# Quadrant swap of a matrix by HBM-to-HBM copies: a short first DMA and a small-packet last DMA on each queue

## Chip, cores, metric

One core of a Trainium2 chip. Times are device microseconds of that core. The runs of one job share a chip. The kernel before took 811.68 us in the median of the first three runs (811.56 to 812.05).

## The reference

```python
def setup_inputs():
    return {"x": np.random.randn(8192, 8192).astype(np.float32)}

def reference(x):
    return np.fft.ifftshift(x)
```

With even sizes this swaps the four quadrants: the upper left one with the lower right one, the upper right one with the lower left one. No arithmetic is done: 268.44 MB are read from HBM and 268.44 MB written.

## The kernel before

```python
STEP = 8
hr, hc = R // 2, C // 2
dims = [[STEP * C, hr // STEP], [1, hc]]        # 512 half rows of 16 KB, every eighth row
for c in range(STEP):
    for col in (0, hc):
        for eng, r0, h in ((nc.sync, 0, col), (nc.scalar, hr, hc - col)):
            eng.dma_start(
                out=bass.AP(out.tensor, out.offset + (r0 + c) * C + h, dims),
                in_=bass.AP(x.tensor, x.offset + (hr - r0 + c) * C + hc - h, dims),
            )
```

SP's queue (q1 in the profile) writes the upper half of the output, ACT's queue (q10) the lower half, 16 DMAs of 8 MB each. No data passes through SBUF. A few words that come again: an issue is the instruction with which SP or ACT hands a DMA to its queue; a packet is what one of the 16 DMA engines moves at a time, here one half row of 16 KB; a completion count is the 4-byte packet with which an engine reports that its share of a DMA is done; landing is when all 16 have; the plateau is the steady rate in the middle of the run.

## Time and profile before

| of the first trace of the kernel before | |
|---|---|
| time, median of 3 unprofiled runs | 811.68 us |
| the profiled execution itself | 823.08 us, span 821.3 us |
| DMA engines' busy share | over 0.9 in 39 of 40 slices |
| 16 KB packet, mean (packet records) | 801 ns, never under 608 |
| first packet / last packet's end | 2.10 / 820.11 us |

The lines themselves stand in the prediction. Read them in three steps: which of the 16 DMA engines' time is empty (the DMA row), how much of the span lies before the first and after the last packet (the stretches), and whether a wait for an earlier DMA keeps an engine from its next packet (the packet records: each packet starts about 4 ns before the one ahead of it ends, so none does).

### The profile page before, as it was taken

Reading aid. Unit: us, or ns where it says so; the run is one execution under the profiler, and the core shown is the slowest. Engines: PE = TensorE matmul, PEld = TensorE weight load, DVE = VectorE, ACT = ScalarE, POOL = GpSimd, SP = SyncE. Lnnn points to the kernel's source line nnn. Section 1 sums busy time; section 2 is a strip of 40 time slices with the busy share of each in tenths; the row PEclk is TensorE's granted clock in tenths of the full one; section 3 lists DMA queues with packets and bytes.
Section 4 is the critical chain, followed back from the end, with each engine's and each line's share of the span. In section 5 each row is a group of like instructions: output and inputs, shape, how many; then the busy total and the mean of one; then the engine's idle time right before and its main releaser. Section 6 shows DMA issues by size and latency. Waiting matters only on the chain. (4 is left out here: it accounts for less than half of the span.)

```text
span 821.3 us, 77 instructions
## 1 busy us (share of the span) xinstructions
POOL 0.2 (0%) x4
## 2 busy tenths in 40 slices
POOL 0000000000000000000000000000000000000000
DMA  9999999999999999999999999999999999999998
GB/s 304 325 328 333 326 325 330 321 329 330 325 330 330 327 328 333 329 330 330 328 328 327 334 325 330 326 326 328 331 329 330 326 332 326 328 324 333 326 328 298
DMA packets 16896, 268.44 MB, mean 327 GB/s; under 512 B 512, under 2 KB 512, under 8 KB 512
## 3 DMA queue, kind: packets, MB, share of 16 engines
q1 hardware_dynamic: 8448, 134.22, 50.2%
q10 hardware_dynamic: 8448, 134.22, 49.7%
HBM read 268.44 MB, written 268.44 MB: 654 GB/s over the span
## 5 line engine op out<-in xcount | busy, mean ns | idle before, releaser
L51 POOL MEMSET const-bfloat16-1.0<- 128x1 bf16 x1 | 0.1, 103 | 0.0
L51 POOL MEMSET const-uint8-127<- 128x1 uint8 x1 | 0.1, 102 | 0.0
L51 POOL MEMSET const-float32-0.0<- 128x1 f32 x1 | 0.1, 99 | 0.2 <-issue 0.2
L51 POOL MEMSET const-float32-1.0<- 128x1 f32 x1 | 0.1, 99 | 0.0
## 6 DMA issues: line engine op xcount, KB each, us to landing
out_dram<-in_x_dram ACTq DMA_DIRECT2D x16, 8192.0 KB, 204.3
out_dram<-in_x_dram SPq DMA_DIRECT2D x16, 8192.0 KB, 204.1
```

Of the source, the lines that this page charges most:

```text
L51: nc = _bacc.Bacc("TRN2", target_bir_lowering=False, num_devices=1)
```

## The change

The intent is to start data moving sooner with a DMA of one row per DMA engine, and to end more evenly with finer packets. Everything between stays.

```diff
-    dims = [[STEP * C, hr // STEP], [1, hc]]
+    def copy(eng, r0, row, n, h, limit=None):
+        dims = [[STEP * C, n], [1, hc]]
+        kw = {"max_dma_last_dim": limit} if limit else {}
+        eng.dma_start(out=..., in_=..., **kw)       # addresses as before, cut here
+
+    full = hr // STEP
     for c in range(STEP):
         for col in (0, hc):
             for eng, r0, h in ((nc.sync, 0, col), (nc.scalar, hr, hc - col)):
-                eng.dma_start(...)
+                if (c, col) == (0, 0):
+                    copy(eng, r0, c, 16, h)
+                    copy(eng, r0, c + 16 * STEP, full - 16, h)
+                elif (c, col) == (STEP - 1, hc):
+                    copy(eng, r0, c, full - 32, h)
+                    copy(eng, r0, c + (full - 32) * STEP, 32, h, 2048)
+                else:
+                    copy(eng, r0, c, full, h)
```

More of the change, by code (lines that the diff above doesn't have):

```diff
@@ L10 @@
 STEP = 8
+PARTS = 16
 @with_exitstack
@@ L27 @@
     hc = C // 2
-    dims = [[STEP * C, hr // STEP], [1, hc]]
+    def copy(eng, r0, row, n, h, limit=None):
+        dims = [[STEP * C, n], [1, hc]]
+        kw = {"max_dma_last_dim": limit} if limit else {}
+        eng.dma_start(
+            out=bass.AP(out.tensor, out.offset + (r0 + row) * C + h, dims),
+            in_=bass.AP(x.tensor, x.offset + (hr - r0 + row) * C + hc - h, dims),
+            **kw,
+        )
+    full = hr // STEP
     for c in range(STEP):
@@ L32 @@
             for eng, r0, h in ((nc.sync, 0, col), (nc.scalar, hr, hc - col)):
-                eng.dma_start(
-                    out=bass.AP(out.tensor, out.offset + (r0 + c) * C + h, dims),
-                    in_=bass.AP(x.tensor, x.offset + (hr - r0 + c) * C + hc - h, dims),
-                )
+                if (c, col) == (0, 0):
[6 more added lines that the diff above has]
+                    copy(eng, r0, c, full, h)
 _INS = ['x']
```

## The prediction

> **What bounds the kernel now.** I read the page first, for which engine is busy, then the stretches at the two ends, then the waits of the queue that closes the program, then the issue times. No compute engine does anything here: the program is 32 copies from HBM to HBM, 16 on each of two queues, so the rows of the DMA engines are the profile.
>
> Of the page of the kernel before (one digit and one GB/s figure for each fortieth of the span, some 20.5 us each):
>
> ```profile
> span 821.3 us, 77 instructions
> DMA  9999999999999999999999999999999999999998
> GB/s 304 325 328 333 326 325 330 321 329 330 325 330 330 327 328 333 329 330 330 328 328 327 334 325 330 326 326 328 331 329 330 326 332 326 328 324 333 326 328 298
> DMA packets 16896, 268.44 MB, mean 327 GB/s; under 512 B 512, under 2 KB 512, under 8 KB 512
> q1 hardware_dynamic: 8448, 134.22, 50.2%
> q10 hardware_dynamic: 8448, 134.22, 49.7%
> HBM read 268.44 MB, written 268.44 MB: 654 GB/s over the span
> ...
> out_dram<-in_x_dram ACTq DMA_DIRECT2D x16, 8192.0 KB, 204.3
> out_dram<-in_x_dram SPq DMA_DIRECT2D x16, 8192.0 KB, 204.1
> ```
>
> The 16 DMA engines are at nine tenths or more in every slice but the last, and the two queues' packet time adds up to 50.2 + 49.7 = 99.9% of 16 engines. 16896 packets are 16384 of 16 KB (one half row each) and 512 of 4 bytes (32 DMAs by 16 engines, the completion counts). Only the first slice (304) and the last (298) are below the plateau of about 328; each loses roughly (328 - 304) / 328 x 20.5 = 1.5 us and (328 - 298) / 328 x 20.5 = 1.9 us. So an edit to the first and last DMA alone has about 3.4 us of profiled time to play for, and part of that is start and finish of the program itself.
>
> The stretches at both ends (length, POOL's busy time, clock, mean busy share of the DMA engines, GB/s; a packet is booked whole to the stretch in which it starts, so a share can exceed 1):
>
> ```profile
> 0.00:2.10 2.10, 0.20 (x4) 1.00 0.00 0
> 2.10:3.50 1.40, 0.00 (x0) 1.00 1.11 269
> 3.50:5.30 1.80, 0.00 (x0) 1.00 0.90 373
> 5.30:8.00 2.70, 0.00 (x0) 1.00 1.08 388
> 8.00:14.00 6.00, 0.00 (x0) 1.00 1.02 347
> ...
> 816.70:818.00 1.30, 0.00 (x0) 1.00 0.97 328
> 818.00:819.00 1.00, 0.00 (x0) 1.00 0.98 328
> 819.00:819.80 0.80, 0.00 (x0) 1.00 0.31 123
> 819.80:820.20 0.40, 0.00 (x0) 1.00 0.00 0
> ```
>
> Nothing moves before 2.10 us; from then on the engines are full until about 819. The packet records say it more finely: all 16 engines take a first packet between 2.10 and 2.70 us, and each starts its next packet about 4 ns before the one before has ended, with no hole in between. A 16 KB packet takes 801 ns in the mean and never under 608; 25% take exactly 611. After the last data packets the 16 engines end between 819.56 and 820.11, in the mean 819.76: the slowest is only 0.36 us behind the mean.
>
> The waits of the queue that closes the program, and the first issues:
>
> ```profile
> SPq L62 <- DMA out_dram<-in_x_dram: 167.2, 2, 118.8
> SPq L33 <- DMA out_dram<-in_x_dram: 133.8, 12, 50.6
> ```
> ```profile
> 0.73 50.48 ACTq L33 DMA_DIRECT2D out_dram<-in_x_dram  x4
> 0.73 45.43 SPq L33 DMA_DIRECT2D out_dram<-in_x_dram  x4
> ```
>
> Each queue issues four DMAs at once (the fourth blocks for 43 to 48 us, so the queue is full), and then waits for the one four back before each of the next 12. With some 200 us from issue to landing, against 51 us of work in one DMA, those waits are far ahead of the data. They cost nothing.
>
> **What the Trainium skill says.** The page "HBM Reference", Specifications, gives about 716 GB/s for an HBM domain. The profile has 654, read and write together: 91% of it, if both tensors lie in one domain, which no view shows. I take it as sign that the plateau is memory's, which the change does not touch. "DMA: Bandwidth & Descriptors", in the section on why a DMA increments its semaphore by 16, says that a hardware-queue DMA uses the largest number of engines up to 16 that divides its slowest dimension. The trace agrees: 512 completion packets for 32 DMAs. New outer sizes are 16, 496 = 16 x 31, 480 = 16 x 30 and 32, so all 16 engines stay in use with equal shares. The same page, "Why small descriptors are slow (HBM only)", gives about 3 cycles of overhead per packet. In the trace a 4-byte completion packet takes 9 ns, about 6 after the overlap: I use 6 ns. "Perfetto Trace Analysis", DMA Instruction, HWDGE, says that the profiled duration of an issue is descriptor generation, not movement. The trace agrees: the first SP issue lasts 0.58 us and its 8 MB land 51 us later.
>
> **The change, part by part.** The bytes, the queues and the order of rows stay. Each queue goes from 16 to 18 DMAs.
>
> 1. First DMA of one row per engine. Before, the first issue runs from 0.73 to 1.31 us (512 rows) and the first packet starts 0.79 later, at 2.10. If generation is proportional to rows, 16 rows take 0.58 x 16 / 512 = 0.02 us and the start is up to 0.56 us earlier. If it is a fixed cost, it is 0. The unblocked 512-row issues last 0.51 to 0.62 us (only DMAs of 512 rows exist, so the split can't be read). I take a bit over half: -0.30 us. This lies straight on the path, since all engines then run full to the end. The second DMA's descriptors come about 0.6 us after the first's; a first packet takes 1.2 to 1.5 us, so no hole opens.
>
> 2. Two more DMAs per queue: 2 x 2 more completion packets per engine, 4 x 6 ns = +0.02 us. Data packets just after a completion packet take 783 ns in the mean, the others 801, so there is no hidden stall. The two more issues run beside full engines: 0.
>
> 3. Last 32 rows of each queue in 2 KB packets. Per engine: 2 rows x 2 queues = 4 packets of 16 KB become 32 of 2 KB, 28 more by 6 ns = +0.17 us. They may also flow less well than 16 KB ones: these 64 rows are 1.05 MB, 3.2 us at 328 GB/s; I allow a further 5%, +0.16.
>
> 4. The end. A finer last packet can shorten the end by what the slowest engine lags, 0.36 us, at most, as rows stay bound to engines; and the drain after the last byte (last completion packet 820.11, its count seen at 820.44) stays. I take -0.15.
>
> Sum: -0.30 + 0.02 + 0.17 + 0.16 - 0.15 = -0.10 us. As the author of such an edit aims at the first and last slice, and as I cannot see the generator's split, I lean a little further to the good side: 811.68 - 0.10 - 0.3 = 811.3 us.
>
> **The rivals.**
> - *Small packets starve the tail.* If an engine can only keep a few packets in flight, 2 KB ones no longer cover the latency (a first packet takes about 0.7 us longer than the 611 floor). For: nothing in this kernel is below 16 KB but the counts. Against: counts flow through in 9 ns without a hole behind them. If the tail ran at half rate, +3.2 us: about 815.
> - *The start or the end is worth all it can be.* -0.56 at the start and -0.36 at the end, small packets free: about 810.8. For: the first slice's 304.
> - *The rows' phase changes the plateau.* With 16 rows split off, the engines' places in the second DMA (496 rows) and in the 480-row one may stand in another relation to each other, which memory may like more or less. These are about 6% of the bytes; a rate 5% up or down on them is 0.06 x 0.05 x 812 = 2.4 us either way, 809 to 814. For: packets of 611 ns beside ones of 925 (75th percentile) show contention, and at the start, with q1 alone (3.4 to 5.3 us), packets take 628 ns in the mean. Against: the plateau moves only between 321 and 334 whatever the drift.
> - *The queues' lead.* q1 is 4 packets per engine ahead at first, and q10 alone ends the run. With short first DMAs they may interleave sooner and end together. q10 alone still moves 328 GB/s, so no gain follows.
>
> **Range and chances.** The three runs spread over 0.5 us. Edges add from -0.9 to about +1 us, the phase up to 2 either way with small weight, a starved tail +3 with about one chance in ten. Predicted 811.3 us, 80% range 809.3 to 813.0. 2% is 16.2 us, five times all that both end slices lose: faster by over 2% has 1%, within 2% 98%, slower 1%.
>
> **What would show it.** First packets at 1.6 to 1.9 us instead of 2.10 would bear out step 1; at 2.1, a fixed issue cost. The packet counts should be 36 x 16 = 576 completion packets and 16384 - 64 + 512 = 16832 of data, 17408 in all, of which 1088 under 8 KB; other counts would mean that the DMAs are cut otherwise than I think. A last slice below 298 GB/s, or 2 KB packets well over 110 ns each, shows the starved tail; a plateau off 328 in slices 2 to 4 or in the last three shows the phase. I am wrong if the time leaves 809.3 to 813.0, above all if the middle of the run moves, where I say nothing changes.

## The result, and the profile after

The changed kernel took 811.86 us in the median of six runs (811.57 to 812.42), the kernel before 811.69 (811.40 to 812.15) in six runs. The ratio is 1.0002, with a 95% interval of 0.9989 to 1.0015: no difference. A ratio is the mean time of one kernel's fast runs over that of the other's fast runs of the same rounds, so it is not quite the ratio of the medians.

From the page of the changed kernel (span; GB/s in 40 slices; packets):

```profile
span 809.9 us, 81 instructions
...
GB/s 298 333 328 334 330 335 333 331 336 330 333 333 333 333 335 333 337 334 329 336 333 335 333 335 333 332 333 333 337 331 335 333 334 330 334 335 329 335 336 299
DMA packets 17408, 268.44 MB, mean 331 GB/s; under 512 B 576, under 2 KB 576, under 8 KB 1088
```

The packet counts are those that the prediction worked out. The two slices that the change aims at have not moved: 298 and 299 against 304 and 298. What differs is what the change does not touch: the slices between are at about 333 instead of 328, and the span is 11 us shorter, while the unprofiled times agree within 0.2 us. So this pair of traces must not be compared for its middle.

The first issues of the changed kernel (start, length of the chain of four issues, both in us), and the waits of SP's queue (total us, times, longest us):

```profile
0.73 2.60 SPq L32 DMA_DIRECT2D out_dram<-in_x_dram  x4
0.73 2.96 ACTq L32 DMA_DIRECT2D out_dram<-in_x_dram  x4
```
```profile
SPq L32 <- DMA out_dram<-in_x_dram: 187.7, 14, 50.1
SPq L75 <- DMA out_dram<-in_x_dram: 116.8, 2, 98.5
```

Four issues now fit into 2.60 us, because the fourth no longer finds the queue full: the four together hold 16 + 496 + 512 + 512 rows where they held 2048. The fifth blocks in its place, for 41.6 us. The first issue by itself, of 16 rows, lasted 0.625 us on SP and 0.632 on ACT; those of 512 rows in the first trace of before lasted 0.582 and 0.591. The first packet starts at 2.12 us, where it was 2.10. The waits are two more, and as the engines stay full beside them (the DMA row has 9 in every slice but the last, as before), they cost nothing.

### The profile page after: what moved, and what is told of

Its sections match the earlier page's. It is cut to its first block, busy times and chain, and to the rows that moved or that the text cites. A ratio compares the mean times of both kernels' runs of the same rounds, so it can differ in the third digit from the quotient of the medians.

```text
span 809.9 us, 81 instructions
## 1 busy us (share of the span) xinstructions
POOL 0.2 (0%) x4
## 2 busy tenths in 40 slices
DMA packets 17408, 268.44 MB, mean 331 GB/s; under 512 B 576, under 2 KB 576, under 8 KB 1088
## 3 DMA queue, kind: packets, MB, share of 16 engines
HBM read 268.44 MB, written 268.44 MB: 663 GB/s over the span
```

## The experiments

**Theory A**: the new first and last DMA do nothing that lasts. An issue costs the same 0.6 us for 16 rows as for 512, the pace is set by memory at about 787 to 800 ns per half row and engine, and the 11 us between the first two traces came with the execution and not with the edit. **Rivals**: the edit made the middle faster (B); start and end cancel (C); small packets cost their overhead wherever they stand (D); each further DMA costs the path (E); the DMA engines themselves set the pace (F).

All twelve runs ended, eleven correct and one wrong. The runs named a1 to a4 were on one chip, b1 to b4 on a second, c1 to c4 on a third.

### a1 to a4: the same kernels again, and each half of the change alone

Edit of a1: none. Edit of a2: none to the changed kernel. Edit of a3: the branch of the last DMA removed from it:

```diff
-                elif (c, col) == (STEP - 1, hc):
-                    copy(eng, r0, c, full - 32, h)
-                    copy(eng, r0, c + (full - 32) * STEP, 32, h, 2048)
```

Edit of a4: the branch of the first DMA removed from it:

```diff
-                if (c, col) == (0, 0):
-                    copy(eng, r0, c, 16, h)
-                    copy(eng, r0, c + 16 * STEP, full - 16, h)
-                elif (c, col) == (STEP - 1, hc):
+                if (c, col) == (STEP - 1, hc):
```

> The kernel before, unchanged, timed against itself. Theory A (the plateau of 328 GB/s in the first trace of before against 333 in that of after is chance of one execution, and the edit does nothing): ratio 1.000 within 0.0015, and a new profile of the same kernel whose span is near 810 us with 16 KB packets near 786 ns in the mean, as in the trace of after. Rival B (the edit made the plateau faster and something unprofiled takes it back): the new profile is again near 821 us with packets near 801 ns.

> The changed kernel once more. Theory A: ratio 1.000 within 0.0015; first packet at 2.1 us, all engines done within 0.3 us of each other at the end. Theory B: span again 11 us under that of before's profile of the same job.

> Only the split of each queue's first DMA. Theory A (an issue costs about 0.6 us whatever its rows): first packet still at 2.1 us and the time within 0.5 us of before. Rival C (the two parts cancel: the short first DMA gains some 0.5 us, the small packets lose as much): 0.5 us faster than before, first packet earlier than 1.9 us.

> Only the last 32 rows of each queue in 2 KB packets. Theory A: 2 KB packets every 80 ns, 640 ns per half row against 611 at the floor and some 790 in the plateau, so within 0.3 us of before. Rival C: 0.5 us slower than before, with the loss in the last 5 us.

| run | median, us | before in the same job | ratio (95%) |
|---|---|---|---|
| a1, before | 824.39 | 824.27 | 1.0000 (0.9987 to 1.0012) |
| a2, after | 824.16 | 824.27 | 1.0001 (0.9987 to 1.0015) |
| a3, first DMA only | 824.54 | 824.27 | 1.0001 (0.9988 to 1.0013) |
| a4, last DMA only | 824.23 | 824.27 | 1.0000 (0.9987 to 1.0013) |

From the page of a1:

```profile
GB/s 299 330 328 329 328 326 330 327 323 330 324 331 331 326 328 329 324 334 326 332 326 331 324 327 329 328 328 332 325 327 328 328 325 331 332 329 329 325 327 295
```

On this chip every kernel takes 824 us, before and after alike, and the middle is at 328 GB/s. On the other two chips before takes 811.5. So the first trace of before (823.08 us) very likely came from a chip like the first, and the trace of after from one like the others; neither record names its chip. That ends rival B: the changed kernel has the 328 plateau too when it runs here. My expectation for a1 was right in its ratio and wrong in its profile, which came out as rival B had said (span 822.3 us, packets 800 ns): I had named chance between executions, where it is the chip. Only a2 on the same chip, and c1 and c2 below, tell the two apart.

Rival C needs half a microsecond each way. The times can't tell that: the interval of 0.13% is about 1 us wide to each side. The first issues and packets can, for the start. SP's first issue in a3 (16 rows), then in a4 (512 rows); the three figures are the shortest, the median and the longest in ns:

```profile
L32 SPq DMA_DIRECT2D out_dram<-in_x_dram x1: 574/574/574, 0.7 to 0.7; - x1
```
```profile
L32 SPq DMA_DIRECT2D out_dram<-in_x_dram x1: 622/622/622, 0.7 to 0.7; - x1
```

So the length of an issue doesn't follow its rows. The first packets come at 2.08 us (a3) and 2.13 (a4). The short first DMA gains nothing there that the end could take back.

### b1, b2: all packets small

Edit, on the kernel before (b1; b2 with 512):

```diff
                 eng.dma_start(
                     out=..., in_=...,
+                    max_dma_last_dim=2048,
                 )
```

> Every half row of the kernel before in 2 KB packets, the change's tail over the whole run. Theory A (memory sets some 800 ns per half row and engine, the engine's own floor of 8 x 80 = 640 ns for 2 KB packets lies under it): within 1% of before, the mean time of eight packets near 800 ns. Rival D (small packets cost their overhead of some 30 ns per half row wherever they stand): 640 / 611, so 4 to 5% slower, and the tail of the change too dear by 0.1 us.

> The same with 512-byte packets, 32 to a half row. If a packet costs about 6 to 8 ns beyond its bytes (estimated from 84 ns against 611 / 8 = 76), the engine's floor is 32 x (19 + 8) - 32 x 4 = about 740 ns: theory A then still within 2% of before; if the floor passes 800 ns, slower in proportion, 5% or more. It shows how far under the memory's pace the 2 KB packets of the change lie.

b1: 821.61 us against 811.60, ratio 1.0128 (1.0113 to 1.0143). b2: 850.9 us, ratio 1.0522 (1.0463 to 1.0580), and its runs spread wide (847.6 to 859.9). From the pages of b1 and b2:

```profile
DMA packets 131584, 268.44 MB, mean 327 GB/s; under 512 B 512, under 2 KB 512, under 8 KB 131584
```
```profile
DMA packets 524800, 268.44 MB, mean 317 GB/s; under 512 B 512, under 2 KB 524800, under 8 KB 524800
```

Both are slower than theory A said (under 1% and under 2%) and far from the full overhead of rival D (4 to 5% for b1). Packets of 2 KB take 84 ns when nothing is in their way, one every 80 ns: 8 x 80 = 640 ns per half row against 607 for 611 less the overlap, 33 ns more. What is paid in the plateau (from the packet records between 100 and 700 us: 329.0 GB/s here, 333.1 in b3 and b4 of the same job) is 16 x 16384 / 329.0 - 16 x 16384 / 333.1 = 797 - 787 = 10 ns. With 512 bytes it is 32 x 23 = 736, 129 ns more, of which 821 - 787 = 34 ns are paid (319.4 GB/s, in b2's fastest run, which is the one traced). The 5.2% of b2 is thus near the "5% or more" of my expectation, but not for its reason, a floor over 800 ns. So the plateau's pace and the packet overhead don't simply overlap, nor do they add: a quarter to a third of the overhead comes through. For the change, whose small packets are 1.05 of 268.44 MB, b1's 10 us shrink to 10 x 0.0039 = 0.04 us.

### b3, b4: how the two queues fall together

Edit of b3, and of b4:

```diff
-(nc.scalar, hr, hc - col)
+(nc.scalar, hr, col)          # b3
+(nc.sync, hr, hc - col)       # b4
```

> The second queue takes the same column half as the first, not the other one, so that what one queue reads no longer has the same offset in its tensor as what the other writes. If the plateau hangs on how the queues' addresses fall together: a change over 1% either way. If not: within 0.3%.

> All 32 DMAs on one queue. The rival that alternating queues slow the packets (628 ns while q1 ran alone at the start, some 800 later): several per cent faster. Theory A (the fast start is only a memory not yet loaded with writes, the plateau is memory's): within 1%, packets near 800 ns.

b3: 811.47 us, ratio 0.9999 (0.9984 to 1.0014). b4: 811.25 us, ratio 0.9996 (0.9981 to 1.0011). Packets took 787 and 788 ns in the mean. Neither which column half the second queue takes nor whether there is a second queue at all matters here. The 628 ns packets at the start, seen while q1 ran alone, are not the pace of a lone queue: in b4 the lone queue settles at 788. The prediction's worry about the queues' lead and about the rows' phase found nothing.

### c1, c2: before and after traced on one chip

> The kernel before once more, for a trace from the same chip as the next one. Theory A: ratio 1.000, nothing before 2.1 us, the engines' ends spread over some 0.5 us.

> The changed kernel on the same chip as the run of before just ahead of it. Theory A (both new edges do nothing, and memory sets the middle): ratio 1.000 within 0.0015, the first packet at 2.1 us, the spans of the two traces within 0.5 us. Rival: the 11 us between the first two traces came with the edit and show up again.

c1: 811.38 against 811.46, ratio 0.9999 (0.9986 to 1.0011). c2: 811.40 against 811.46, ratio 1.0000 (0.9987 to 1.0012). Stretches of the trace of before (c1), then of after (c2); columns as in the prediction:

```profile
3.50:5.30 1.80, 0.00 (x0) 1.00 0.98 410
100.00:700.00 600.00, 0.00 (x0) 1.00 1.00 333
...
806.00:807.00 1.00, 0.00 (x0) 1.00 1.18 393
807.00:807.50 0.50, 0.00 (x0) 1.00 0.28 98
807.50:808.00 0.50, 0.00 (x0) 1.00 0.01 0
808.00:808.50 0.50, 0.00 (x0) 1.00 0.00 0
```
```profile
3.50:5.30 1.80, 0.00 (x0) 1.00 0.97 391
100.00:700.00 600.00, 0.00 (x0) 1.00 1.00 333
...
806.00:807.00 1.00, 0.00 (x0) 1.00 0.96 326
807.00:807.50 0.50, 0.00 (x0) 1.00 0.98 274
807.50:808.00 0.50, 0.00 (x0) 1.00 0.62 209
808.00:808.50 0.50, 0.00 (x0) 1.00 0.09 33
```

On one chip both run at 333 GB/s in the middle, and the spans are 809.1 and 809.9 us: the 11 us are gone. My expectation of spans within 0.5 us was missed: they are 0.73 apart. The end is where they differ, and to the wrong side: the last data packet ends at 807.94 us in before and at 808.69 in after. To put a number on both edges I used the packet records: bytes moved up to a time (each packet counted linearly over its duration), against the plateau's rate. "Start" is 20 us less the time that the bytes moved by then would take at that rate, "end" is the same for the last 20 us before the last packet's end.

| trace | short first DMA | 2 KB tail | first packet, us | start lost, us | end lost, us |
|---|---|---|---|---|---|
| first of before | no | no | 2.10 | 2.03 | 0.33 |
| a1 | no | no | 2.09 | 2.21 | 0.52 |
| c1 | no | no | 2.09 | 2.00 | 0.25 |
| a4 | no | yes | 2.13 | 2.06 | 0.50 |
| a3 | yes | no | 2.08 | 2.31 | 0.31 |
| first of after | yes | yes | 2.12 | 2.55 | 0.48 |
| a2 | yes | yes | 2.13 | 2.07 | 0.90 |
| c2 | yes | yes | 2.14 | 2.02 | 0.91 |

The short first DMA loses 2.24 us in the mean (four traces), the long one 2.08: no gain. The 2 KB tail loses 0.70 us in the mean, the 16 KB tail 0.35: if anything a third of a microsecond dearer, with a spread as large as the difference. Neither is visible in times that scatter by about a microsecond.

Two more expectations were missed here. I had the engines' ends within 0.3 us of each other in a2 and spread over some 0.5 us in c1. Read from the last 16 completion counts on ACT's queue, which closes the run, they lie 1.53 and 0.83 us apart.

### c3: the short DMA throughout

Edit, on the kernel before:

```diff
-    dims = [[STEP * C, hr // STEP], [1, hc]]
+    dims = [[STEP * C, 16], [1, hc]]
...
+            for k in range(0, hr, 16 * STEP):       # r = c + k in place of c
```

> The change's short first DMA made the rule: every DMA of the kernel before cut into 32 of 16 rows, 1024 DMAs, in the same order of rows as far as a DMA deals its rows out in turn. Theory A (issue at 0.6 us a DMA and queue runs beside full engines; two DMAs issued in 0.6 us bring 32 rows, 1.6 us of work): within 1% of before, with 31 x 32 more completion counts per engine by 6 ns = 6 us as the most they could cost. Rival E (each DMA costs the path its issue or its completion): 512 x 0.6 = 307 us is the issue alone per queue and hidden, but four DMAs in flight per queue are 8 rows per engine, 6.4 us, against about 3 us from issue to landing; if landing under load takes over 6.4 us the engines run dry and the time goes up by several per cent.

812.47 us against 811.46, ratio 1.0011 (0.9996 to 1.0027). From the page (packets, issues) and the waits of SP's queue of c3:

```profile
DMA packets 32776, 268.57 MB, mean 331 GB/s; under 512 B 16384, under 2 KB 16384, under 8 KB 16384
...
out_dram<-in_x_dram SPq DMA_DIRECT2D x512, 256.0 KB, 6.3
```
```profile
SPq L36 <- DMA out_dram<-in_x_dram: 532.4, 502, 2.5
```

1024 DMAs where there were 32 cost 1.0 us, which the interval can't tell from nothing, and 2.2 at its upper end. Rival E falls: a DMA takes 6.3 us from issue to landing, SP waits 532 us in total, and the engines are still full, as four DMAs stay in flight per queue. (Eight half rows per engine at 0.78 us are 6.2 us, so the 6.3 is the time that the DMAs ahead take.) The completion counts should have cost 992 more per engine x 6 ns = 6 us. They are nearly all taken back: the mean 16 KB packet is 780.3 ns against 786.4 in c1, and 1024 x 6.1 ns = 6.2 us. So the engines' time for the counts was not time that the data lacked. It is not that the packet next after a count is served faster: those took 782 ns in c3 and the others 775.

### c4: HBM written and hardly read

Edit, on the kernel before:

```diff
+    t = pool.tile([128, hc], mybir.dt.float32)
+    nc.sync.dma_start(out=t[:], in_=...)            # 2 MB, once
...
-                in_=bass.AP(x.tensor, ...)
+                in_=t[:],                           # 128 rows per DMA, 128 DMAs
```

> Wrong on purpose: all of the output is written from one tile in SBUF, so HBM is written and hardly read. Theory A (reading and writing HBM together sets some 790 to 800 ns per packet): packets come down to the floor of about 611 ns, 1024 x 0.61 = 625 us and a total near 632 us, 22% faster. Rival F (the DMA engines themselves, or their queues, set the plateau): packets stay near 790 ns and the time near that of before.

641.89 us, ratio 0.7911 (0.7900 to 0.7921). Its output is wrong, which doesn't matter for the time. From its page:

```profile
GB/s 328 426 426 426 426 426 426 426 426 426 426 426 426 426 426 427 428 425 429 426 426 428 425 429 427 425 427 426 426 426 426 428 426 426 427 427 425 427 428 377
...
HBM read 2.10 MB, written 268.44 MB: 423 GB/s over the span
```

The same engines, on the same two queues, take 618 ns for a 16 KB packet, near the floor of 608 to 611. Rival F falls: the engines and queues have a fifth in hand, and HBM as the source of the copy is what takes it. Whether it is reading and writing together that takes it, as theory A has it, or reading alone, was not tried over a whole run. Over some 4 us c4's own load into SBUF only reads HBM: from 3.04 us to its end at 7.2 us every packet took 608 or 611 ns. But the copy's packets too began near the floor (628 ns between 3.4 and 5.3 us of the first trace), so a few microseconds don't settle it. Nor was another distance between rows tried: the copies and c4's writes step by 256 KB, c4's load by 32 KB. The total is 10 us above my estimate, of which the load ahead of the first write is 7. One thing came by the way: the load into SBUF, of 128 rows, took 0.38 us to issue and its first packet started at 1.76 us, sooner than any of the copies inside HBM, of whatever size.

No experiment pointed to a version clear of both kernels. The lowest, b4 with one queue, is at 811.25 us inside the interval of no difference.

## Why the prediction was right or wrong

The time was in the range (811.86 us, range 809.3 to 813.0) and "within 2%" was right, for the reason given: all engines are full, and the edges are short. That the plateau is memory's was argued then; c4 shows that it is not the engines' or the queues', and memory is what is left, though not shown as such. The hit on the time says little of the steps: with all of them at zero it would have lain in the range too. The gain of 0.4 us that the point estimate held was not seen, and an interval from 0.9 us faster to 1.2 us slower could not have shown it. So the steps are judged from the traces.

- **Step 1, -0.30 us, was wrong.** It supposed that a good half of an issue's time follows the rows. In this copy inside HBM it did not: the first issues of 16 rows last 0.57 to 0.64 us (a3, c2, c3), those of 512 rows 0.58 to 0.62 (a1, a4), in no order of size. The first packet comes at 2.08 to 2.14 us in all eight traces of the table, whatever the first DMA holds. This was the larger of the two named gains; its right value is 0.
- **Step 2, +0.02 us, was right** in counts (576 and 17408, as measured) and too careful in cost: c3 has 992 more counts per engine and pays about a sixth of their time (1.0 us of 6, itself not clear of noise).
- **Step 3, +0.33 us, is neither borne out nor refuted.** A further packet costs an engine (640 - 607) / 7 = 5 ns with nothing in its way, near the 6 assumed; the mean 2 KB packet took 99 ns in the first trace of after and 106 in c2 (115 on SP's queue there), where an eighth of a 787 ns packet is 98. That is not the "well over 110" of a starved tail. b1 puts the cost at the plateau at 0.04 us. The end as a whole came out 0.35 us dearer in the mean of four traces, where steps 3 and 4 together had +0.18.
- **Step 4, -0.15 us, was not borne out.** It also rests on a wrong reading. The prediction has the engines ending between 819.56 and 820.11 us; by the 16 last completion counts they end between 818.98 and 820.11, so six engines were missed, and the slowest lags the mean by 0.60 us and not 0.36. With the 16 KB tail the last counts lie 0.83 to 1.14 us apart (the first trace of before, a1, a3, c1), with the 2 KB tail 0.93 to 1.53 (that of after, a2, a4, c2; there SP's queue ends nearly as late, so a count need not be its engine's end). No levelling shows.
- **The lean of -0.3 us** had no measurement behind it, and none was found.
- **What I overlooked**: the first trace's own execution took 823.08 us beside timed runs of 811.68. The 801 ns and 328 GB/s of the working were very likely a slower chip's. No step hung on it, since the edges are short; a prediction on the middle would have gone wrong by 1.5%.
- **The rivals**: starved tail and phase did not happen (plateau 333.1 GB/s in c1, 333.2 in c2). The weight of the phase was half of what it should have been: two DMAs of 496 and two of 480 rows are 12% of the 16384 half rows, not 6%, so the swing to allow for was 4.8 us and not 2.4. The lead did shrink as foreseen: q10's first packet comes at 2.92 us instead of 5.31, with no gain.

Left open: whether the 0.35 us at the end is real, as it would need some dozen traces on one chip, why one chip's plateau is 1.5% under that of two others, and which property of HBM, or of the way to it, holds the copy at 787 ns a packet.

## What to carry to other kernels

When the DMA engines are full from the first packet to the last, cut nothing at the edges before you have counted what they lose: here 2 us at the start, which a first DMA of 16 rows didn't shorten against one of 512, and 0.3 us at the end. Look for the resource that sets the packet's duration (take away the reads, and see whether the packet gets shorter) before you rearrange issues, queues or packets. And compare a profile's own time with the timed runs, and traces only when they come from one chip: two traces here differed by 11 us for a change that did nothing.

## What the Trainium skill lacked or had wrong

- "DMA: Bandwidth & Descriptors", Latency and other measured facts, gives about 600 ns to the first byte for a hardware queue, without saying from where it counts. Here, between HBM tensors, the issue alone lasted 0.57 to 0.64 us for 16 rows as for 512, and the first 16 KB packet started 1.35 to 1.41 us after the issue's start; from HBM to SBUF (c4) it was 0.38 and 1.03 us. The page gives no issue time by rows or by memory for Trainium2.
- "Perfetto Trace Analysis", DMA Optimizations, says that going from 2 KB transfers to 4 or 8 KB can improve throughput dramatically. In this HBM-to-HBM copy, 2 KB packets in place of 16 KB ones cost 1.3% (b1), and 512-byte ones 5.2% (b2). If the page means whole DMAs and not packets, c3 is the nearest: 256 KB in place of 8 MB, 0.1% and not clear of noise.
- "HBM Reference" gives one core's stream at about 425 GB/s, which c4 confirms for writes (426), but nothing for a copy inside HBM; what the skill has on such copies, in "DMA: Bandwidth & Descriptors", starts at rows 512 KiB apart. Here, with rows 256 KB apart and 16 KB packets, it was 326 to 332 GB/s read and as much written at once, 653 to 664 in sum over the span.
- No page that I read says how far chips differ: 824.27 us against 811.60 and 811.46 for one kernel on three chips, 1.6%.
